# Two-layer hybrid encoder in float32: operand loads moved ahead at the turn to the output projection, one step run ahead of its preparations, and three VectorE and ScalarE jobs spread

## The chip, the cores and the metric

The kernel runs on one core of one Trainium2 chip. A core has TensorE (PE, matmuls; PEld is its weight load), VectorE (DVE), ScalarE (ACT), GpSimd (POOL) and SyncE (SP, which here only issues DMAs). Data lie in SBUF (128 partitions), matmuls accumulate in PSUM banks. The metric is the device time of one execution in microseconds (us); lower is better.

## The reference

One layer is computed on 2048 tokens of width 1024, all in float32: a conditioned RMS norm, one input projection, two kinds of attention with eight heads of 64 each, an output projection with a gated residual, a second norm, and an MLP with a gated residual.

```python
h = rmsnorm(x, g_norm1) * (1 + sc1) + sh1
q_sb, k_sb, v_sb, q_ca, k_ca, v_ca = split(h @ w_in)
o_sb = stick_breaking_attention(q_sb, k_sb, v_sb)             # strictly causal, 8 heads
o_ca = chunked_relpos_attention(rms(q_ca), rms(k_ca), v_ca)   # own chunk + 8 before, 8 heads
x = x + gt1 * (concat(o_sb, o_ca) @ w_o)
h = rmsnorm(x, g_norm2) * (1 + sc2) + sh2
x = x + gt2 * (square(relu(h @ w1)) @ w2)
```

## The kernel before, in words

**Number format.** TensorE multiplies a rounded form of float32. Each operand is therefore split into a rounded high part (a cast, mostly on ACT) and a low part (source minus high, mostly on DVE), and `mm3` (line 211) makes each product from three matmuls: high by high, high by low, low by high. In the MLP the weight is the stationary side, so the third of the three is the first to need the weight's low part.

**Stages.** The tokens stand in four blocks `g` of 512 columns (reversed in time). First come the input projections. Then attention runs unit by unit: SB units (stick breaking; per head and pair of blocks) and CA units (chunked softmax; per head and block), in the order blocks 2 and 3, then 1, then 0. A unit has four steps. In each step DVE scans or reduces one score tile, POOL makes the weights from it, and eight steps later PE transposes the weights, ACT and DVE split them, and PE multiplies them with the values into a bank `acc`. Between these matmuls `fill` (line 1291) puts a share of independent matmuls: projections still to be made, and the output projection `outproj` (line 1155) of blocks 3 to 1. `later.tick()` (line 1401) runs delayed jobs once a step; `soon`, `urgent` and `heavy` are lists of jobs of which each step takes a few.

**Head copies.** When a unit's last value matmul is out, `finish` (line 774) copies one half of `acc` to `otmp` on ACT and puts a second copy, to `o`, on the urgent list; after both POOL adds them. There are two `acc` banks, so the second-next unit's first value matmul needs the two copies. On the last two steps of an SB unit on the diagonal (`short`, line 1391) only jobs beyond the third are taken.

**Norm diagonal.** For blocks 2 and 3 the second norm is made during attention (`finish_row`, line 1186): squares are added up, brought into columns, raised to the power -1/2 on POOL, and then `spread` (line 1215) multiplies the identity with the columns on DVE (`ndgm`), `third` (line 1228) spreads the result over the partitions with matmuls (`prm`) and copies it out.

**The turn.** After attention, four rows of block 1's output projection are left (`row`, line 2097; PE writes `po`). Then eight steps `Mixed` (line 1976; PE writes `pso`) make block 0's output projection. Their moving operands are the eight parts of the attention result, `opm`, loaded from `scr_m[0, k]` by `fetch` (lines 1986 and 2105 to 2112): four ahead of the rows, two after the second row and two after the third, all issued by SP. Parts 4 to 6 are stored by POOL's queue and part 7 by ACT's, shortly before (`keep`, line 798). In the same stretch `right_blocks` (line 1505, called by `some`, line 2091) loads four tiles `ty` (and later `cy`) of the residual stream, multiplies them with the norm on DVE, scales and shifts them on ACT, and forms seven operand tiles `h` of the Strassen-like products of the MLP's first layer. These jobs are written out by hand, block by block (lines 2105 to 2128).

**The MLP.** Its products are lists of steps: `First` (line 1589; seven products, order 1, 5, 6, 3, 7, 2, 4 for each pair of weight tiles), `Second` and `Outer`. The last loop (line 2133) goes through the steps: it first prepares the operands of later steps while there is room for eight tiles, then runs the step's listed jobs (`at`), and then the step's own matmuls. At step 7 it prepares the first two operands of step 8 (`firsts`, shown as `opr`) and makes the four weight sums (`First.fetch`, line 1619; tiles `s`, `ts`, `w`). Step 8 is the first step of `First`; its result is copied by ACT into a second bank (`ps_s<-ps`), on which step 10 goes on. For the second half of the tokens the four weight sums of the first pair are made together six steps before its first step (line 2063).

**Order.** ACT, DVE, POOL and PE instructions, and SP's DMAs from the turn on, keep the order in which the program writes them.

Of the kernel before, what the change touches and what calls it, by code (L numbers as in the profile page):

```python
# [9 lines left out]
F32 = mybir.dt.float32  # L10
# [3 lines left out]
ALU = mybir.AluOpType  # L14
# [4 lines left out]
P = 128  # L19
# [5 lines left out]
KT = D // P  # L25
# [54 lines left out]
def encoder_kernel(ctx, tc, xs, c, g1, g2, w_in, w_first, w_rest, gqk, bias, w_o, w1, w2, w_ada, b_ada, out):  # L80
# [58 lines left out]
    later = Later()  # L139
# [597 lines left out]
    if True:  # L737
# [448 lines left out]
        def finish_row(g, n, ps, xr):  # L1186

            residual(g, n, ps, xr)
            if g < 2 and drain:
                return  # L1190
            stores.pop()()
            if g < 2:
                return

            def square():
                sq = rows[g] if n == 0 else op.tile([P, TB], F32, tag="otmp", name=f"sq{g}_{n}")
                act.activation(sq, xr, AF.Square)
                if n:
                    soon.append(lambda: add(sq))

            def add(sq):
                pool.tensor_tensor(rows[g], rows[g], sq, op=ALU.add)
                if n == KT - 1:
                    later.add(14 if g == 3 else 3, second)

            def second():
                pv = norm_columns(dense, rows[g], f"m{g}")

                def powers():
                    y = norm_powers(op, pv, f"m{g}")  # L1210
                    later.add(2, lambda: spread(y))

                later.add(1, powers)

            def spread(y):
                dg = op.tile([P, TB], F32, tag="otmp", name=f"ndgm{g}").rearrange("p (a b) -> p a b", b=P)

                def part(i):
                    dve.tensor_tensor(
                        dg[:, i : i + 2], ident.unsqueeze(1).to_broadcast([P, 2, P]),  # L1220
                        y[:, i : i + 2].unsqueeze(2).to_broadcast([P, 2, P]), op=ALU.mult,
                    )

                part(0)
                later.add(1, lambda: part(2))
                later.add(3, lambda: third(dg))

            def third(dg):
                pr = dense.tile([P, TB], F32, tag="ps", name=f"prm{g}")
                for i in range(4):  # L1230
                    pe.matmul(pr[:, i * P : (i + 1) * P], ones, dg[:, i, :], start=True, stop=True)
                later.add(1, lambda: dve.tensor_copy(rows[g], pr))

            if n == 0:
                rows[g] = rp.tile([P, TB], F32, tag="r", name=f"r{g}")
            soon.append(lambda: heavy.append(square))
# [123 lines left out]
        for i in range(len(steps) + LAG):  # L1360
            if i % STEPS == 0:
                if i // STEPS + AHEAD < len(units):
                    load(units[i // STEPS + AHEAD])
            vi = i - VST
            if vi >= 0 and vi % STEPS == 0 and vi // STEPS < len(units):
                units[vi // STEPS].load_values()
            front, fs = steps[i] if i < len(steps) else (None, 0)
            back, bs = steps[i - LAG] if i >= LAG else (None, 0)
            done = list(soon)
            soon.clear()  # L1370
            js = []
            if back is not None:
                nb = len(back.blocks)
                js = range(nb * bs // STEPS, nb * (bs + 1) // STEPS)
            for j in js:
                back.transposes(j)
            if front is not None:
                front.soft1(fs)
            while first:
                first.pop(0)()  # L1380
            for j in js:
                back.parts(j)
                late.append((back, j))
            if front is not None:
                front.soft2(fs)
            for job in done:
                if hasattr(job, "bank"):
                    heavy.append(job)
                else:
                    job()  # L1390
            short = front is not None and not front.ca and front.diag and fs > 1
            n = len(urgent) + len(heavy)
            for _ in range(max(0, n - 3) if short else min(n, 1 + (n > 3))):
                (urgent or heavy).pop(0)()
            while len(late) > AVLAG:
                value(*late.pop(0))
            if i + 1 < len(steps):
                u, st = steps[i + 1]
                u.scores(st)
            fill(shares[i], turns.get(i, 0))  # L1400
            later.tick()
# [27 lines left out]
    if True:  # L1429
# [37 lines left out]
        def at(n, job):  # L1467
            jobs.setdefault(n, []).append(job)
# [507 lines left out]
        class Mixed(Step):  # L1976
# [6 lines left out]
                self.tiles = 0 if at else KT  # L1983
                self.frees = KT if at == KT - 1 else 0

            def fetch(self, *ks):
                for k in range(*ks):
                    m = Mixed.parts[k] = opp.tile([P, 2, TB], F32R, tag="op", name=f"opm{self.g}_{k}")
                    sp.dma_start(m.bitcast(F32), scr_m[self.g, k])

            def load(self):
                g, n = self.g, self.n
# [29 lines left out]
        for mb in (1, 0):  # L2022
            begin = len(steps)
            steps += [First(mb, j, i) for j in range(NP) for i in OUTER]
            end = len(steps)
            for j in range(NP):
                f = steps[begin + 7 * j]
                if mb:
                    second_sums(j, begin + 7 * j + 2)
                    if j >= HP:  # L2030
                        narrow_sums(2, j - HP, begin + 71 + 5 * (j - HP))
                else:
                    if j < 12:
                        outer_sums((7, 5, 3)[j // 4], j % 4, begin + 9 * j - 2)
                    if j < HP:
                        for i, n in ((3, 4), (2, 5), (7, 4), (4, 5)):
                            at(begin + 7 * j + n, lambda i=i, f=f: f.other(i))
                    else:
                        narrow_sums(4, j - HP, begin + 65 + 5 * (j - HP))
                if j > mb:  # L2040
                    at(begin + max(7 * j - 13, 2 if mb else -6), f.load)
                if j > mb or mb and j:
                    for m in range(4):
                        at(begin + (m + 1 if mb and j == 1 else 7 * j - 9 + (m if j > 1 else 0)), lambda f=f, m=m: f.fetch(m))
            if mb:
                norm2(1, begin + 18)
                norm2(0, begin + 48)
                for k in range(HK):
                    begins = end + 6 * k
                    pieces = right_blocks(0, k, kept if k % 2 else temp)  # L2050
                    for n, m in ((0, 0), (4, 4), (5, 5), (6, 6), (7, 7), (8, 7), (9, 7), (10, 7), (11, 7), (12, 7)):
                        at(begins + n, pieces[m])
                for i in PLAIN:
                    plain(1, i)
                for n in range(end, len(steps), 2):
                    at(n - 7 - max(0, end + 4 - n) // 2, steps[n].load)
                rest = len(steps)
                lent = lambda nm: rp.tile([P, TB], F32, tag="r", name=nm)
                for n in range(HK):
                    update(1, n, rest + 4 + 12 * n, lent, True)  # L2060
            else:
                at(begin - 8, steps[begin].load)
                at(begin - 6, steps[begin].fetch)

        def plain_loads(f, leads):
            for m in range(0, NP, 2):
# [35 lines left out]
                stores.pop(0)()  # L2102
            return force(left)

        steps[0].fetch(0, KT // 2)
        row()
        row()
        some(0, 0)
        steps[0].fetch(KT // 2, KT - 2)
        row()  # L2110
        some(0, 1)
        steps[0].fetch(KT - 2, KT)
        row()
        some(0, 2)
        some(1, 0)
# [15 lines left out]
        ahead = iter(steps[1:])  # L2131
        nxt = next(ahead)
        for n, s in enumerate(steps):
            while nxt is not None and ready - used + nxt.tiles <= 8 and nxt.ready():
                nxt.prepare()
                ready += nxt.tiles
                nxt = next(ahead, None)
            for m in (0, 1) if n == 0 else (n + 1,):
                if m < KT:
                    steps[m].load_row()  # L2140
            for job in jobs.get(n, ()):
                job()
            if n == KT - 1:
                firsts = spare.tile([P, 2, 2, TB], F32R, tag="r8", name="opr")
                steps[KT].prepare(firsts[:, 0])
                steps[KT].fetch(0)
                steps[KT + 1].prepare(firsts[:, 1])
                for m in range(1, 4):
                    steps[KT].fetch(m)
            s.run()  # L2150
            used += s.frees
            later.tick()
        later.flush()
# [42 lines left out]
```

## Time and profile before

| what | value |
|---|---|
| time, median of 3 runs | 2514.77 us (2513.28 to 2515.25) |
| profiled execution, its own time | 2516.38 us |
| its span in the profile | 2514.6 us |
| busy share of the span: PE, DVE, ACT, POOL | 99%, 81%, 61%, 31% |
| attention ends, PE goes on with `po` alone | 1268.66 us |
| first `Mixed` matmul | 1290.50 us |
| first `First` matmul (step 8) | 1336.53 us |
| first `First` matmul of the second half | 1736.00 us |

The span lacks what lies around the profiled program, here 1.8 us. All times inside the execution are counted from the span's start. In the timeline rows the first number is the start, the second the time until the last of the merged instructions ends, `xN` their count, and a bracket the idle time of the engine before them with what ended it. In the rows of waits stand the total, the number of times and the longest one.

### The profile page before, as it was taken

How to read it: one execution, taken by the hardware profiler on the slowest of the kernel's cores; microseconds unless marked ns; L12 is line 12 of the kernel's file. 1: busy time of each engine (PE TensorE's matmuls, PEld its weight loads, DVE VectorE, ACT ScalarE, POOL GpSimd, SP SyncE). 2: the span in 40 equal slices, each digit the busy share in tenths (PEclk: the TensorE clock that was granted, in tenths of full speed). 3: DMA queues.
4: the chain of work that ended last, by engine and by line, in shares of the span. 5: the costliest groups of instructions: out<-in, count | busy, mean ns of one | idle time of the engine just before them, and what ended most of it. 6: DMA issues, size and time to landing. Idle time of an engine off the chain costs nothing.

```text
span 2514.6 us, 39505 instructions
## 1 busy us (share of the span) xinstructions
PE 2498.9 (99%) x12364; PEld 2094.8 (83%) x12364; DVE 2027.7 (81%) x3567; ACT 1526.4 (61%) x2928; POOL 787.1 (31%) x1174
## 2 busy tenths in 40 slices
PE   9999999999999999999999999999999999999999
PEld 8888888888888888888888888888888888888887
DVE  7656777897799888999858777779877759799998
ACT  6333424778876686666755555567555546577765
POOL 4330154777776677776710000000000000010100
PEclk9999999999999999999999999999999999999999
DMA  9879978789888788866786878996998996888982
GB/s 357 333 297 362 356 269 291 233 262 311 268 262 260 237 259 254 268 195 216 213 323 245 299 285 305 330 351 191 327 323 269 315 363 262 320 249 282 303 280 84
DMA packets 295970, 704.71 MB, mean 280 GB/s; under 512 B 32080, under 2 KB 88400, under 8 KB 284112
## 3 DMA queue, kind: packets, MB, share of 16 engines
q1 hardware_dynamic: 287552, 684.35, 79.3%
q0 software_dynamic: 6768, 13.11, 2.9%
q10 hardware_dynamic: 1440, 4.72, 0.5%
q8 instruction: 98, 1.61, 0.3%
q14 instruction: 112, 0.92, 0.1%
HBM read 473.99 MB, written 228.07 MB: 279 GB/s over the span
## 4 chain that ended last, share of the span: by engine, by line
PE 86%; DVE 5%; DMA 4%; ACT 2%; issue 1%; POOL 0%; SPq 0%; DVEq 0%; ACTq 0%; POOLq 0%
PE ps L42 24%; PE ps_s L42 15%; PE pt L42 11%; PE acc L42 7%; PE wt L42 7%; PE pf L42 6%; PE z L42 5%; PE po L42 4%; PE pq L42 3%; PE cz L42 2%; PE ct L42 1%; DMA scr_t<-twn 1%; DMA hw<-in_w_dram 1%; DVE h L42 1%; DMA opm<-scr_m 1%
## 5 line engine op out<-in xcount | busy, mean ns | idle before, releaser
L42 ACT CAST wth<-wt 128x512 fp32r<-128x512 f32 (+3 forms) x544 | 257.5, 484 | 173.3 <-PE wt L42 160.7
L42 PE MATMUL ps<-h,opw 128*128 128x512 f32 x1512 | 358.6, 389 | 0.0
L42 POOL TENSOR_TENSOR b<-p 128x512 f32<-128x512 f32 (+1 forms) x320 | 291.9, 912 | 155.7 <-DVE p L42 95.6
L42 DVE TENSOR_TENSOR wtl<-wt,wth 128x512 fp32r<-128x512 f32 (+3 forms) x544 | 291.2, 547 | 60.7 <-ACT wth L42 56.2
L42 PEld LDWEIGHTS ps<-h,opw 128*128 128x128 f32 x1512 | 283.6, 188 | 58.9
L42 PE MATMUL pt<-w,ht 128*128 128x512 f32 x1248 | 288.0, 391 | 0.0
L42 PE MATMUL ps_s<-h,opw 128*128 128x512 f32 x1152 | 277.6, 390 | 1.5 <-ACT ps_s L42 1.0
L42 PEld LDWEIGHTS pt<-w,ht 128*128 128x128 f32 x1248 | 232.9, 188 | 47.5
L42 DVE TENSOR_TENSOR_SCAN p<-z,p,zero 128x512 f32<-128x512 f32 x192 | 245.3, 1279 | 20.6 <-ACT z L42 14.9
L42 PEld LDWEIGHTS ps_s<-h,opw 128*128 128x128 f32 x1152 | 215.7, 188 | 47.9 <-ACT ps_s L42 1.4
L42 ACT CAST opr<-r 128x512 fp32r<-128x512 f32 x280 | 174.3, 623 | 118.2 <-PE ps L42 65.6
L42 PE MATMUL acc<-wth,v 128*128 128x512 f32 (+3 forms) x544 | 221.3, 410 | 1.1 <-ACT o L42 1.1
L42 PE MATMUL ps<-opr,ol 128*128 128x512 f32 x960 | 220.3, 389 | 0.0
L42 PEld LDWEIGHTS ps<-opr,ol 128*128 128x128 f32 x960 | 180.1, 188 | 37.8 <-DVE opr L42 0.4
L42 ACT ACTIVATE z<-z 128x512 f32<-128x512 f32 (+1 forms) x320 | 166.6, 521 | 54.3 <-PE z L42 49.9
L42 DVE TENSOR_TENSOR opr<-r,opr 128x512 fp32r<-128x512 f32 x280 | 185.7, 684 | 13.7 <-ACT opr L42 12.5
L42 PE MATMUL acc<-wtl,v 128*128 128x512 f32 (+3 forms) x544 | 185.6, 347 | 0.0
L42 PE MATMUL z<-k,q 128*128 128x512 f32 (+3 forms) x640 | 182.8, 367 | 1.0 <-DVE p L42 0.9
L42 POOL DMA_DIRECT2D scr_x<-txu x12 | 10.4, 866 | 547.7 <-ACT txu L42 545.9
L42 PE MATMUL ps<-oph,opv 128*128 128x512 f32 x768 | 175.7, 390 | 1.2 <-DVE oph L42 0.9
L42 PE MATMUL wt<-ident,b 128*128 128x128 f32 x1088 | 170.7, 272 | 0.4 <-DVE p L42 0.4
L42 PEld LDWEIGHTS ps<-oph,opv 128*128 128x128 f32 x768 | 143.9, 188 | 32.6 <-DVE oph L42 1.4
(238 smaller groups left out, 5062.1 us busy)
## 6 DMA issues: line engine op xcount, KB each, us to landing
r<-scr_hid SPq DMA_DIRECT2D x80, 512.0 KB, 7.4
q<-scr_q SPq DMA_DIRECT2D x128, 256.0 KB, 5.2
w<-in_w_dram SPq DMA_DIRECT2D x64, 512.0 KB, 5.7
k<-scr_k SPq DMA_DIRECT2D x240, 128.0 KB, 4.6
v<-scr_v SPq DMA_DIRECT2D x120, 256.0 KB, 4.6
wa<-in_w_ada_dram SPq DMA_DIRECT2D x48, 512.0 KB, 6.3
ow<-scr_wo SPq DMA_DIRECT2D x24, 1024.0 KB, 6.7
l<-scr_t SPq DMA_DIRECT2D x20, 1024.0 KB, 8.6
```

The lines of the kernel that those rows point to most:

```text
L42: return lambda *x, **y: self.tc.keep_in_program_order(f(*x, **y))
```

## The change

Five edits:

1. **Norm diagonal**: four multiplications of 128x128 in four steps in a row, where there were two of 128x256 in two; `third` comes one step later.
2. **Head copies**: the rule `short` does not hold while the front unit belongs to block 0 and an urgent job waits.
3. **Turn**: parts 0 to 5 of `opm` are fetched by SP ahead of all rows, parts 6 and 7 by ACT's queue directly after that.
4. **First product**: the matmuls of step 8, and the copy behind them, are written ahead of that step's preparations and jobs.
5. **Weight sums**: the second half's first four sums are made one a step, on the steps six to three ahead of its first step.

```diff
@@ finish_row, spread
                 def part(i):
-                    dve.tensor_tensor(
-                        dg[:, i : i + 2], ident.unsqueeze(1).to_broadcast([P, 2, P]),
-                        y[:, i : i + 2].unsqueeze(2).to_broadcast([P, 2, P]), op=ALU.mult,
-                    )
+                    dve.tensor_tensor(dg[:, i], ident, y[:, i : i + 1].to_broadcast([P, P]), op=ALU.mult)
 
                 part(0)
-                later.add(1, lambda: part(2))
-                later.add(3, lambda: third(dg))
+                for i in range(1, 4):
+                    later.add(i, lambda i=i: part(i))
+                later.add(4, lambda: third(dg))
@@ attention loop
-            short = front is not None and not front.ca and front.diag and fs > 1
+            short = front is not None and not front.ca and front.diag and fs > 1 and not (front.g == 0 and urgent)
@@ Mixed
-            def fetch(self, *ks):
+            def fetch(self, *ks, queue=sp):
                 for k in range(*ks):
                     m = Mixed.parts[k] = opp.tile([P, 2, TB], F32R, tag="op", name=f"opm{self.g}_{k}")
-                    sp.dma_start(m.bitcast(F32), scr_m[self.g, k])
+                    queue.dma_start(m.bitcast(F32), scr_m[self.g, k])
@@ steps of the second half
                 at(begin - 8, steps[begin].load)
-                at(begin - 6, steps[begin].fetch)
+                for m in range(4):
+                    at(begin - 6 + m, lambda f=steps[begin], m=m: f.fetch(m))
@@ the turn
-        steps[0].fetch(0, KT // 2)
+        steps[0].fetch(0, KT - 2)
+        steps[0].fetch(KT - 2, KT, queue=act)
         row()
         row()
         some(0, 0)
-        steps[0].fetch(KT // 2, KT - 2)
         row()
         some(0, 1)
-        steps[0].fetch(KT - 2, KT)
         row()
@@ last loop
         for n, s in enumerate(steps):
+            if n == KT:
+                s.run()
             while nxt is not None and ready - used + nxt.tiles <= 8 and nxt.ready():
...
-            s.run()
+            if n != KT:
+                s.run()
             used += s.frees
             later.tick()
```

## Prediction

> **What bounds the kernel now.** I read the page's busy shares first, then PE's waits, then the timelines around the places that the diff touches.
>
> ```profile
> PE 2498.9 (99%) x12364; PEld 2094.8 (83%) x12364; DVE 2027.7 (81%) x3567; ACT 1526.4 (61%) x2928; POOL 787.1 (31%) x1174
> ```
> ```profile
> PE pso L42 <- DMA opm<-scr_m: 1.9, 2, 1.6
> ...
> PE acc L42 <- ACT o L42: 1.1, 1, 1.1
> PE ps_s L42 <- ACT ps_s L42: 1.0, 1, 1.0
> PE ps L42 <- DVE oph L42: 0.9, 1, 0.9
> PE z L42 <- DVE p L42: 0.9, 2, 0.5
> PE cz L42 <- DVE cols L42: 0.7, 1, 0.7
> ```
>
> PE is busy 99% of the span, and the change removes no matmul. Only PE's holes can be won, and these six waits are the ones it aims at. A wait row counts idle time only; a hole is better measured from start to start, with the pace of matmuls that nothing holds up:
>
> ```profile
> 1268.66 22.00 PE L42 MATMUL po<-fx,ow 128*128 128x512 f32 x96
> 1290.50 4.29 PE L42 MATMUL pso<-opm,ow 128*128 128x512 f32 x18
> ...
> 1336.53 5.81 PE L42 MATMUL ps<-h,opr 128*128 128x512 f32 x24
> 1343.30 3.04 PE L42 MATMUL ps_s<-h,opw 128*128 128x512 f32 x12 [0.96 <-ACT ps_s L42]
> ```
>
> From 1268.66 to 1290.50 are 96 matmuls: 0.2275 us each. The eight `Mixed` steps have 192 of them, 43.68 us, so they could end at 1334.18; `First` begins at 1336.53, a hole of 2.35. Its two steps of 12 end at 1341.99, the next begins at 1343.30: 1.31. With 1.1 for the head copies, 0.5 and 0.7 for the two diagonals, and 1.58 for the weight sums (below), 7.5 us stand at the touched places. That is the most that can be won, 0.30%.
>
> **The change part by part.**
>
> **Head copies: -1.1.** One place fits the new condition: block 0's first diagonal unit, with a CA unit's copies still urgent.
>
> ```profile
> 953.28 0.58 ACT L42 COPY otmp<-acc 64x512 f32<-64x512 f32 x1
> ...
> 955.18 0.58 ACT L42 COPY o<-acc 64x512 f32<-64x512 f32 x1
> ```
>
> PE's wait of 1.1 ends with the second copy (955.76). The rule releases both two steps earlier, some 4 us, well ahead of PE's need at about 954.7. The copies stay two of 0.58 us. ACT is 61% busy and hides them; without that cover each could hold up one sigmoid by 0.58, which reaches PE only if DVE's scan behind it has no spare time. Bounds: -1.3 and -0.5.
>
> **Norm diagonal: -0.2.** Here a row speaks against the change.
>
> ```profile
> 1038.35 1.15 DVE L42 TENSOR_TENSOR ndgm<-ident,nym 128x256 f32<-128x256 f32 x1
> ...
> 1208.68 1.24 DVE L42 TENSOR_TENSOR ndgm<-ident,nym 128x256 f32<-128x256 f32 x1
> ```
> ```profile
> 1038.18 1.04 POOL L42 TENSOR_TENSOR b<-p 128x512 f32<-128x512 f32 x1
> ```
> ```profile
> 1208.39 1.25 POOL L42 TENSOR_TENSOR e<-e,cols 128x640 f32<-128x640 f32 x1 [1.68 <-DVE wtl L42]
> ```
>
> The instruction takes 1.15 and 1.24 us. Both times it ends 0.28 us after POOL's instruction does (1039.50 after 1039.22; 1209.92 after 1209.64). So the cost is waiting for POOL, and 0.28 is the work. Half the width saves about 0.14 of each of the first two parts, which fall on the same steps as before; the other 0.8 to 1.1 stays. Two more parts follow, each of which can wait up to 1.25 again. The holes of 0.5 and 0.7 thus shrink by about 0.14 each, of which I leave 0.1 to the extra parts: -0.2. The ends: -1.2 (0.5 + 0.7) if no part waits, and +0.9 if the two extra parts of one diagonal wait some 1.1 each and DVE has only 1.3 to spare before a score bank is late. The matmuls `prm` only move one step.
>
> [...]
>
> **Turn: +0.7.** What SP does there:
>
> ```profile
> 1260.72 1.85 SPq L42 DMA_DIRECT2D opm<-scr_m  x4
> ...
> 1283.85 0.33 SPq L42 DMA_DIRECT2D txr<-in_xs_dram  x1
> 1284.24 1.85 SPq L42 DMA_DIRECT2D ty<-scr_x  x4
> ```
> ```profile
> 1275.90 0.33 ACTq L42 DMA_DIRECT2D scr_m<-os  x1
> ```
> ```profile
> SPq L42 <- DMA scr_m<-os: 9.1, 1, 9.1
> ```
> ```profile
> ow<-scr_wo SPq DMA_DIRECT2D x2, 1024.0 KB, 7.4
> ...
> scr_m<-os ACTq DMA_DIRECT2D x1, 512.0 KB, 7.9
> ```
>
> A `txr` waits 9.1 us for ACT's store of part 7, which it does not read: 1275.90 + 7.9 = 1283.8. In program order it is the eighth DMA of SP and ACT behind that store (four `opm`, `ow`, `txr`, `ow`, `txr`). I read this as a ring of eight completion counters: each DMA waits for the one eight before it. After the change the order is store 7, parts 0 to 5, parts 6 and 7 (ACT), `ow`, `txr`, `ow`, `txr`, then four `ty`. The four `ty` stand eight behind parts 4, 5, 6 and 7. The fourth `ty` now waits for part 7 to land, and part 7 waits for its store at 1283.8.
>
> ```profile
> L42 SPq DMA_DIRECT2D ty<-scr_x x4: 424/430/432, 1284.2 to 1285.7; - x4
> ...
> DMA to landing us min/median/max: 3.5/4.8/5.4
> ```
> ```profile
> opm<-scr_m SPq DMA_DIRECT2D x8, 512.0 KB, 7.4
> ```
> ```profile
> 1290.32 1.44 DVE L42 TENSOR_TENSOR ty<-ty,r 128x512 f32<-128x512 f32 x2 [0.38 <-DMA ty<-scr_x]
> ...
> 1328.19 1.29 DVE L42 TENSOR_TENSOR h<-cy,h 128x512 fp32r<-128x512 f32 x2 [1.05 <-ACT h L42]
> ...
> 1336.32 0.68 DVE L42 TENSOR_TENSOR opr<-w,opr 128x512 fp32r<-128x512 f32 x1
> ```
>
> Part 7, issued near 1283.9, lands after 3.5 us (the fastest `ty`, half its bytes) to 7.4 (the median `opm`, in full traffic); I take 4.4, nearer to the quiet end since the traffic has been moved ahead. 1288.3, then 3.4 for the fourth `ty`: 1291.7. Before, the last two multiplications ended at 1290.32 + 1.44 = 1291.76 and one takes 0.7, so DVE began with the fourth near 1291.0. So the operand chain starts 0.7 later.
>
> Does that count? From 1291 to 1337 DVE and ACT hand each other the 28 tiles `h`; DVE's idle stretches end with ACT (the row at 1328.19 shows the longest, 1.05), ACT's with DVE, none with PE. The chain ends with `opr` at 1336.32 + 0.68 = 1337.00. PE's third matmul of `First`, the first to need it, falls at 1336.53 + 2 x 0.2275 = 1336.99. PE and the chain meet there with nothing to spare. So when the 2.35 of waiting for `opm` go, PE arrives at 1334.2 and waits for `opr` instead, some 3 us. The gain is hidden anyway; the chain's shift is what remains. Also moved: SP now stands still for part 5 until the store of it lands, which POOL issues near 1262 (about 1270 by the 7.9 of a store), with `ow` behind it, issued near 1271 and landed near 1278.5 by its 7.4; PE needs it at 1268.66 + 48 x 0.2275 = 1279.6. If it is late, the 3 us that PE waits later cover it. ACT's queue stands still for part 7 until 1283.8; behind it wait the scalings of `ty`, of which the first comes near then, since `ty` is issued from 1275 on; so this costs nothing. Bounds: -2.35 (the chain keeps up) and +2.5 (part 7 takes 6.2).
>
> **First product: -1.2.**
>
> ```profile
> 1339.66 1.35 ACT L42 CAST opw<-ts 128x512 fp32r<-128x512 f32 x2 [1.41 <-PE ps L42]
> ...
> 1342.67 0.57 ACT L42 COPY ps_s<-ps 128x512 f32<-128x512 f32 x1
> ```
>
> Step 8's product is ready at 1336.53 + 12 x 0.2275 = 1339.26, but its copy stands behind five casts and ends at 1343.24. Written first, it ends near 1339.9, two us before PE needs it, and the hole of 1.31 goes. The price: the casts start 0.3 later. Step 10's weight is due at 1342, with its cast done near 1340.5 and DVE's low part by 1342.2, just ahead of its third matmul at 1342.4; I leave 0.1 for that. Bounds -1.3 and -0.6. It holds whether or not `First` itself begins later.
>
> **Weight sums: -1.5.**
>
> ```profile
> 1726.88 0.68 DVE L42 TENSOR_TENSOR s<-w 128x512 f32<-128x512 f32 x1
> ...
> 1729.53 0.68 DVE L42 TENSOR_TENSOR oph<-hw,oph 128x512 fp32r<-128x512 f32 x1
> ...
> 1736.16 1.28 DVE L42 TENSOR_TENSOR opw<-ts,opw 128x512 fp32r<-128x512 f32 x2
> ```
> ```profile
> 1724.64 4.69 PE L42 MATMUL ps<-oph,opv 128*128 128x512 f32 x20
> 1730.27 5.89 PE L42 MATMUL ps<-oph,opv 128*128 128x512 f32 x23 [0.93 <-DVE oph L42]
> 1736.00 5.60 PE L42 MATMUL ps<-h,opw 128*128 128x512 f32 x24
> ```
>
> Four sums stand in DVE's queue ahead of `oph`. 1724.64 + 20 x 0.2275 = 1729.19, PE goes on at 1730.27 (1.08), and 23 matmuls later another 0.50 is lost. With one sum ahead instead of four, `oph` starts 3 x 0.66 = 2.0 us sooner, at 1727.6. Each later step's low parts then have one sum less of a lead: 1.3 and 0.7 us sooner, and none from the fourth step on, where PE is 1.58 earlier. There the weights of the third and fourth product of `First` are ready at 1737.44, and PE begins the third at 1736.00 + 24 x 0.2275 = 1741.46, so 4.0 us of lead pay for the 1.58. POOL is idle here, so no sum waits. -1.5; bounds -1.6 and -0.8.
>
> **Sum.** -1.1 - 0.2 + 0.7 - 1.2 - 1.5 = -3.3 us. The profiled execution took 2516.38, 1.6 above the median; 2513.1 for it, and 2514.77 - 3.3 = **2511.5** for the median. 0.2% is 5.0 us, about what a measurement of this kernel can tell from no change.
>
> **The rivals.**
>
> *The chain keeps up at the turn* (0.22). If the fourth `ty` comes some 2 us sooner, or the chain has spare time that I don't see, the 2.35 is won: -6.35, 2508.4. For it: the traffic is moved into a stretch where PE and ACT are quiet. Against it: the store of part 7, which nothing moves, still lands ahead of part 7 and `ty`.
>
> *The diagonal's extra parts wait for POOL and PE feels it* (0.15). +0.9 in place of -0.2: 2512.6. For it, all of the long `ndgm` rows; against it, DVE's spare time on later steps.
>
> *The turn makes it slower than before* (0.08). The store of part 7 shares the DMA engines with all that is moved ahead of it.
>
> ```profile
> 1268.00:1274.00 6.00, 6.00 (x30) 4.85 (x29) 1.07 (x3) 2.18 (x5) 4.47 (x4) 1.00 1.02 401
> 1274.00:1280.00 6.00, 6.00 (x28) 4.99 (x27) 0.88 (x2) 0.50 (x1) 1.29 (x1) 1.00 0.92 310
> ```
>
> In these two windows they are 1.02 and 0.92 busy. Two parts, a `txr` and two `ty`, 1.75 MB, go ahead of it; at 401 GB/s that is 4.4 us. If all of it is served before the store, the chain starts 0.7 + 4.4 = 5.1 later: -4.0 + 5.1 = +1.1, 2515.9. It decides from 3.3 us of delay of the store.
>
> *The copies don't come sooner* (0.05), because the urgent list is empty on those steps: 2512.6.
>
> **Chances and range.** The forecast has 0.50, from 2510 to 2513.5. The range takes in the first rival at its lower end and stops short of the third: 2508.3 to 2514.9. Faster by over 0.2% (below 2509.7) is most of the first rival and the forecast's edge: 0.25; slower by over 0.2% needs more than the third rival gives: 0.03; within, 0.72.
>
> **What would show it.** PE's wait for `opm` gone and one of about 3 us for `opr` at `First`'s begin; the fourth `ty` issued when part 7 lands; no wait for `o`, `ps_s` and `oph`; the four narrow `ndgm` ending just after POOL's instructions, with PE's waits for `p` and `cols` nearly as before. I am wrong if `First` begins 2 us earlier in the span, counted from the last attention matmul, or if narrow `ndgm` take 0.2 to 0.3 us.

## The result, and the profile after

| | kernel before | changed kernel |
|---|---|---|
| median (range) of 22 runs each | 2514.5 us (2511.33 to 2516.20) | 2516.92 us (2513.92 to 2520.13) |
| profiled execution, its span | 2516.38, 2514.6 | 2515.57, 2513.9 |

The ratio is 1.0013, 95% interval 1.0007 to 1.0019: the changed kernel is 2.4 us slower. The forecast was 3.3 us faster.

The two profiled executions alone would say 0.7 us faster. Each is one draw from a spread of 5 to 6 us, and the first lies above its median, the second below. So the medians give the total, and the profile gives the places.

PE's waits in the changed kernel (total, times, longest):

```profile
PE po L42 <- DMA ow<-scr_wo: 5.5, 1, 5.5
```

Of the six waits that the change aimed at, four (`opm`, `o`, `ps_s` behind ACT, `oph`) are gone, and those for `p` and `cols` are shorter. At the head of the list stands one that the kernel before did not have: the third of block 1's last four rows, row 6, waits 5.5 us for its weight tile `ow`. PE's timeline at the turn:

```profile
1266.83 11.12 PE L42 MATMUL po<-fx,ow 128*128 128x512 f32 x48
1283.47 12.83 PE L42 MATMUL po<-fx,ow 128*128 128x512 f32 x48 [5.52 <-DMA ow<-scr_wo]
1296.13 16.48 PE L42 MATMUL pso<-opm,ow 128*128 128x512 f32 x72
...
1339.65 5.60 PE L42 MATMUL ps<-h,opr 128*128 128x512 f32 x24
1345.09 2.88 PE L42 MATMUL ps_s<-h,opw 128*128 128x512 f32 x12
```

PE's rows at the begin of the second half:

```profile
1719.75 15.58 PE L42 MATMUL ps<-oph,opv 128*128 128x512 f32 x68
1735.16 5.60 PE L42 MATMUL ps<-h,opw 128*128 128x512 f32 x24
```

Read from stage to stage against the rows of before:

- Attention ends at 1266.83, before at 1268.66: -1.83.
- From there to the begin of `First` 72.82 us, before 67.87: +4.95. The wait is 5.7 from start to start. Behind it 48 matmuls take 12.66 (1283.47 to 1296.13), which at 0.2275 would be 10.92: another 1.74. From this 7.4 the 2.35 for `opm` come off, since `pso` now runs through.
- From there to the second half 395.51, before 399.47: -3.96. No hole is left at step 10 (1345.09 stands 24 x 0.2267 behind 1339.65) and none for `oph`.
- From there to the end 778.74, before 778.6.

Why `ow` came late is read in SP's timeline of the changed kernel:

```profile
1270.05 0.32 SPq L42 DMA_DIRECT2D opm<-scr_m  x1
1276.97 0.32 SPq L42 DMA_DIRECT2D ow<-scr_wo  x1
...
1278.88 4.79 SPq L42 DMA_DIRECT2D ty<-scr_x  x4
```

ACT's timeline beside it:

```profile
1274.08 0.33 ACTq L42 DMA_DIRECT2D scr_m<-os  x1
1274.67 2.60 ACTq L42 DMA_DIRECT2D opm<-scr_m  x2
```

That store among the DMAs from 1255 to 1292 (count, KB each, median us from issue to landing):

```profile
scr_m<-os ACTq DMA_DIRECT2D x1, 512.0 KB, 2.8
```

And SP's waits in the same window:

```profile
SPq L42 <- DMA scr_m<-os: 14.8, 2, 8.3
...
SPq L42 <- DMA ow<-scr_wo: 4.8, 2, 2.9
```

ACT issues the store of part 7 at 1274.08. It lands 2.8 later, at 1276.9, and in that moment SP issues `ow`. SP waits twice for a store of `scr_m`, 14.8 us in all: 8.3 ahead of part 5, which reads what POOL stored, and 6.5 ahead of `ow`, which reads nothing of the kind. So, by the reading that the prediction gave the 9.1 us of `txr` (each DMA waits for the one eight before it), `ow` stands eighth behind the store of part 7. The last row bears it out: the fourth `ty` waits 2.9 us for `ow`, its own place eight before, and is issued at 1283.35 as `ow` lands.

The clock in the same stretch (window, PE busy and count, PEld, DVE, ACT, POOL, then PEclk, DMA share, GB/s):

```profile
1278.00:1283.00 5.00, 0.00 (x0) 0.00 (x0) 0.00 (x0) 0.00 (x0) 0.00 (x0) 0.72 0.97 346
1283.00:1287.00 4.00, 3.53 (x8) 2.81 (x9) 0.75 (x1) 0.00 (x0) 0.00 (x0) 0.50 1.02 409
1287.00:1291.00 4.00, 4.00 (x19) 3.30 (x18) 2.22 (x4) 1.74 (x3) 0.00 (x0) 0.99 0.97 321
```

When `ow` lands, PE goes on at half its clock (0.50) until 1287: 8 matmuls in the 3.5 us in which 15 fit. That is the 1.74.

### The profile page after: what moved, and what is told of

Read it like the earlier page. It is cut to its first block, busy times and chain, and to the rows that moved or that the text cites. A ratio compares the mean times of both kernels' runs of the same rounds, so it can differ in the third digit from the quotient of the medians.

```text
span 2513.9 us, 39512 instructions
## 1 busy us (share of the span) xinstructions
PE 2497.9 (99%) x12364; PEld 2096.0 (83%) x12364; DVE 2028.7 (81%) x3571; ACT 1525.7 (61%) x2928; POOL 787.0 (31%) x1174
## 4 chain that ended last, share of the span: by engine, by line
PE 89%; DVE 4%; DMA 3%; ACT 2%; issue 1%; SPq 0%; POOL 0%; DVEq 0%; ACTq 0%; POOLq 0%
PE ps L42 24%; PE ps_s L42 15%; PE pt L42 11%; PE acc L42 8%; PE wt L42 7%; PE pf L42 6%; PE z L42 5%; PE po L42 5%; PE pq L42 3%; PE cz L42 2%; PE pso L42 2%; PE ct L42 1%; DMA hw<-in_w_dram 1%; PE px L42 1%; DMA scr_t<-twn 0%
## 5 line engine op out<-in xcount | busy, mean ns | idle before, releaser
L42 PE MATMUL po<-fx,ow 128*128 128x512 f32 x576 | 164.2, 397 | 5.5 <-DMA ow<-scr_wo 5.5
```

The lines of the kernel that those rows point to most:

```text
L42: return lambda *x, **y: self.tc.keep_in_program_order(f(*x, **y))
```

## The experiments

**The theories.** *A*: the late `ow` is the loss, through its place in the ring. *B*: another edit lost the time, or something that the profiled execution does not show. Each kernel ran on a chip with runs of the kernel before beside it; "against before" means those. The intervals are some 2.2 us to either side, so differences below that are read from the profiles.

### The changed kernel without the turn's edit, and the turn's edit alone

```diff
-        steps[0].fetch(0, KT - 2)
-        steps[0].fetch(KT - 2, KT, queue=act)
+        steps[0].fetch(0, KT // 2)
         row()
         row()
         some(0, 0)
+        steps[0].fetch(KT // 2, KT - 2)
         row()
         some(0, 1)
+        steps[0].fetch(KT - 2, KT)
```

> The changed kernel with the turn's edit taken back; the other four edits stay. Theory A (the weight tile ow of row 6 stood eight DMAs behind the store of part 7, and its late landing costs all that the other edits gain and more): no wait for ow, 96 matmuls of po again at 0.2275 us, the wait for opm of about 1.6 us is back, attention still ends 1.8 us sooner than in the kernel before; -1.8 - 1.2 - 1.5 = -4.5 against the kernel before, some 2510.0 us; 6 to 7 us below the changed kernel's median of 2516.9 if its stall is usually as long as in its profile. Theory B (the loss comes from one of the four other edits, or from something that the profiled execution does not show): 2514.5 us or more, less than 2 us below the changed kernel.

Measured 2511.15 us, -2.8 against before (2513.91), ratio 0.9991 (0.9982 to 1.0000). That is 5.8 below the changed kernel's median, and 5.2 when each of the two is counted against its own runs of the kernel before.

For the turn's edit alone on the kernel before:

> The kernel before with the turn's edit alone. Theory A: a wait of PE for ow of 4 to 6 us in the third row of po, then some 3.4 us of matmuls at 0.43 us each; no wait for opm; stall 5.7 + slow matmuls 1.7 - opm 2.35 = +5.0, about 2519.5 us. Theory B: within 1.5 us of the kernel before, 2513 to 2516.

Measured 2519.89 us, +6.0, ratio 1.0025 (1.0015 to 1.0034), with the wait for `ow` at the same row:

```profile
1285.70 13.70 PE L42 MATMUL po<-fx,ow 128*128 128x512 f32 x48 [5.55 <-DMA ow<-scr_wo]
```

The turn's edit costs 5 to 6 us with or without the others, so theory B falls. The 48 matmuls behind the wait take 13.70 us here, 12.83 in the changed kernel and 11.12 at full pace, so this second loss varies: 2.6 us here, 1.7 there. The other four together bring 2.8, not the 4.0 of the prediction's terms. Where the rest is, the profile of the kernel without the turn's edit shows. PE:

```profile
1333.95 5.78 PE L42 MATMUL ps<-h,opr 128*128 128x512 f32 x24
1339.57 2.88 PE L42 MATMUL ps_s<-h,opw 128*128 128x512 f32 x12
...
1346.60 3.02 PE L42 MATMUL ps_s<-h,opw 128*128 128x512 f32 x12 [1.43 <-ACT cp L42]
1349.46 2.88 PE L42 MATMUL ps<-h,opw 128*128 128x512 f32 x12
```

ACT in the same kernel:

```profile
1343.13 0.62 ACT L42 CAST opw<-w 128x512 fp32r<-128x512 f32 x1 [2.40 <-DMA w<-in_w_dram]
1345.44 0.62 ACT L42 CAST opw<-ts 128x512 fp32r<-128x512 f32 x1 [1.69 <-DVE ts L42]
1345.97 0.58 ACT L42 COPY cp<-ps_s 128x512 f32<-128x512 f32 x1
```

The hole at step 10 is gone, and two products later PE waits 1.43 us for the copy `cp`, which stands behind two casts, of which the first waits for a load of `w`.

### Without the turn's edit and without that of the first product

The diff is against the kernel without the turn's edit.

```diff
-            if n == KT:
-                s.run()
...
-            if n != KT:
-                s.run()
+            s.run()
```

> Without the turn's edit and without that of the first product (head copies, diagonal and weight sums alone). Theory A (the first product's 1.3 us came back at the fourth product, where PE waits 1.4 us for a copy cp that stands behind casts on ACT): the wait of 1 us for ps_s of step 10 is back at 1340, that of 1.4 us for cp at 1345 is gone; 2511.2 us as without the turn's edit alone, within 0.5. Rival (the edit of the first product is worth its 1.2 us, and the wait for cp has another cause): the wait for cp stays too, 2512.4 us.

Measured 2510.67 us, -3.7 against before (2514.37), ratio 0.9987 (0.9978 to 0.9996). The span is 2509.3, with the edit 2509.2. PE's rows:

```profile
1332.99 6.01 PE L42 MATMUL ps<-h,opr 128*128 128x512 f32 x24
1339.98 3.01 PE L42 MATMUL ps_s<-h,opw 128*128 128x512 f32 x12 [0.99 <-ACT ps_s L42]
...
1345.69 3.02 PE L42 MATMUL ps_s<-h,opw 128*128 128x512 f32 x12
1348.55 2.88 PE L42 MATMUL ps<-h,opw 128*128 128x512 f32 x12
```

The wait at step 10 is back, the one for `cp` is gone, and the span is the same. From `First`'s begin to the product behind the one that needs `cp` PE takes 15.56 us (1332.99 to 1348.55), with the edit 15.51 (1333.95 to 1349.46). Written ahead, the first product brings PE sooner to the next late thing, and no more.

### Parts 4 to 7 on POOL's queue

```diff
-        steps[0].fetch(0, KT - 2)
-        steps[0].fetch(KT - 2, KT, queue=act)
+        steps[0].fetch(0, KT // 2)
+        steps[0].fetch(KT // 2, KT, queue=pool)
```

> The changed kernel, but parts 0 to 3 of opm are fetched by SP as in the kernel before and parts 4 to 7 by POOL's queue, so ow of row 6 stands fifth and ow of row 7 seventh behind the store of part 7. Theory A: neither ow waits, PE waits neither for ow nor for opm. By the second half of the prediction's step (chain of h tiles meets PE with nothing to spare) PE then waits 2 to 4 us for opr at the begin of First, and the time is that of the kernel without the turn's edit, within 1 us: about 2510. By the rival (the chain keeps up) no wait for opr over 0.5 us and 2.3 us less, about 2507.7. If ow still comes late by 5 us, theory A's order of DMAs is wrong: about 2517.

Measured 2514.03 us, ratio 1.0001 (0.9992 to 1.0010). No wait for `ow`, none for `opm`. `First` begins like this:

```profile
1334.96 0.73 PE L42 MATMUL ps<-h,opr 128*128 128x512 f32 x2 [2.45 <-ACT opr L42]
1336.43 6.79 PE L42 MATMUL ps<-h,opr 128*128 128x512 f32 x22 [0.73 <-DVE opr L42]
```

A window of the same kernel:

```profile
1336.00:1340.00 4.00, 3.57 (x9) 2.85 (x10) 3.27 (x6) 0.62 (x1) 0.00 (x0) 0.57 0.17 66
```

The 2.45 and 0.73 us of waiting for `opr` are the "some 3 us" of the prediction. The rival by which the chain keeps up is out. The time is not that of the kernel without the edit, though, but 2.9 us more. The window shows a cost that nobody had counted: PEclk 0.57, with a DMA share of 0.17. Behind this wait, too, matmuls run at half pace, for (1 - 0.57) x 4 / 0.5 = 3.4 us: from 1336.43 to 1343.06 stand 22 matmuls, 6.63 us in place of 5.0, so it costs 1.6. Between the two profiles (2511.5 and 2509.2), counted from start to start at 0.2267 a matmul, that makes 3.6 for `opr` and 1.6 of half pace, less 1.6 for `opm`, 1.7 for `cp` and 0.2 of small holes, which are gone: +1.7 of the 2.3.

### One place in the ring

```diff
-        steps[0].fetch(KT - 2, KT, queue=act)
+        steps[0].fetch(KT - 2, KT, queue=pool)
```

The kernel above changed the place of `ow` and the early traffic at once. This one leaves six parts early.

> The changed kernel with one thing different: parts 6 and 7 are fetched by POOL's queue and not by ACT's. Parts 0 to 5 stay ahead on SP, with all their traffic. That takes one DMA out of the ring between the store of part 7 and ow of row 6, so ow stands seventh behind it and the txr after it eighth. Theory A (the place in the ring alone makes ow late): ow of row 6 is issued between 1266 and 1271 and lands by 1278, no wait for it over 0.5 us; now txr waits for the store, so ow of row 7 is issued right after the store's landing, near 1277.5, lands near 1284 and costs a wait of up to 1.5 us near 1283; then some 3 us for opr. About 2514, like the kernel with parts 4 to 7 on POOL. Rival (the six early parts fill the DMA engines and ow is late for that): a wait of 3 us or more for ow of row 6 stays, 2516 to 2517.

Measured 2514.87 us, ratio 1.0004 (0.9994 to 1.0014). SP in this kernel:

```profile
1269.02 0.38 SPq L42 DMA_DIRECT2D ow<-scr_wo  x1
1278.96 0.33 SPq L42 DMA_DIRECT2D txr<-in_xs_dram  x1
1279.39 0.56 SPq L42 DMA_DIRECT2D ow<-scr_wo  x1
```

PE:

```profile
1277.75 5.72 PE L42 MATMUL po<-fx,ow 128*128 128x512 f32 x24 [0.19 <-DMA ow<-scr_wo]
1287.29 8.58 PE L42 MATMUL po<-fx,ow 128*128 128x512 f32 x24 [3.82 <-DMA ow<-scr_wo]
```

With the same six parts ahead, row 6's `ow` is issued 8 us sooner and PE waits 0.19. `txr`, now the eighth, waits for the store, and row 7's `ow` behind it in SP's queue comes 3.82 us late. The stall moved by one row as the ring moved by one place: the place is the cause, the traffic of the early parts is not. The size was off: the store landed 1.4 us later than assumed and `ow` took 7.8 us to land, not 6.5, so the stall is 3.8, not up to 1.5. Two things went otherwise than expected and nearly cancel. Behind the stall 24 matmuls take 8.58 us, the 24 before them 5.72, so the slower pace costs another 2.9. And PE then waits for no `opr`, where 3 us were expected.

### PE kept busy through the wait

```diff
+                if g == 1 and n == 6:
+                    for _ in range(22):
+                        pe.matmul(ps, mx[0][:, 0, :P], mx[0][:, 0, :], start=True, stop=True)
```

> The changed kernel with 22 extra matmuls (22 x 0.2275 = 5.0 us) on tiles that lie in SBUF already, written ahead of row 6 of block 1's output projection into the bank that the row then begins anew; the outputs are those of the reference. They fill PE's wait for ow. If the half pace behind the wait comes from the idleness: PEclk stays at 1.00 and the matmuls behind ow's landing run at 0.2275 us; First begins 1.4 to 1.8 us sooner against ow's landing; about 1.7 us below the changed kernel, 2515.2. If the half pace comes from the traffic in the same microseconds: 0.43 us again, and the time as the changed kernel, 2516.9. If ow lands earlier than in the profiled execution, the extra matmuls cost up to 5 us themselves.

Measured 2514.77 us, 2.15 below the changed kernel's median (1.6 when each is counted against its own runs of the kernel before); against before 1.0008 (0.9999 to 1.0017). Two windows of this kernel:

```profile
1278.00:1283.00 5.00, 5.00 (x23) 3.81 (x21) 0.00 (x0) 0.00 (x0) 0.00 (x0) 1.00 1.00 391
1283.00:1287.00 4.00, 2.99 (x14) 2.49 (x14) 0.75 (x1) 0.00 (x0) 0.00 (x0) 1.00 1.00 380
```

PE's rows from `ow`'s landing on:

```profile
1284.02 11.18 PE L42 MATMUL po<-fx,ow 128*128 128x512 f32 x48 [1.01 <-DMA ow<-scr_wo]
...
1338.55 5.60 PE L42 MATMUL ps<-h,opr 128*128 128x512 f32 x24
```

`ow` lands within 0.7 us of the changed kernel's. The clock stays at 1.00 in the same DMA traffic (share 1.00), and `First` begins 54.5 us behind the landing, in the changed kernel 56.2 (1283.47 to 1339.65). So in this stretch idleness, not traffic, makes the half pace (0.50 in the changed kernel); it costs 1.7 us here, and 22 useless matmuls buy it back.

### The kernel before once more

> The kernel before, unchanged, run once more with a profile of its own. Its profiled execution took 2516.4 us, 2.4 us over the median of 32 runs (2513.9). If this lies in the execution and not in the profile: the median is again 2513.9 within 0.7 us, and a second profile shows a span of 2511 to 2513 with smaller holes at the places where the first one has 1.1 us and more (the copies at 954, opm at 1294 to 1297, the weight sums at 1729, ps_s at 1962).

Measured 2514.13 us (ratio 0.9998, 0.9990 to 1.0007), span 2511.1, 3.5 below that of the first profile. PE's rows in this second profile:

```profile
1295.17 0.96 PE L42 MATMUL pso<-opm,ow 128*128 128x512 f32 x3 [1.59 <-DMA opm<-scr_m]
1296.42 13.32 PE L42 MATMUL pso<-opm,ow 128*128 128x512 f32 x51 [0.29 <-DMA opm<-scr_m]
...
1336.78 5.60 PE L42 MATMUL ps<-h,opr 128*128 128x512 f32 x24
1342.22 2.88 PE L42 MATMUL ps_s<-h,opw 128*128 128x512 f32 x12
...
1732.72 5.60 PE L42 MATMUL ps<-h,opw 128*128 128x512 f32 x24
```

One window of it:

```profile
1296.00:1300.00 4.00, 3.71 (x10) 2.87 (x10) 3.91 (x8) 1.39 (x3) 0.00 (x0) 0.57 1.06 407
```

The waits for `opm` are those of the first profile, 1.59 and 0.29. Here, but not there, the clock halves behind them (13.32 for 51 matmuls, there 11.86). PE then comes late enough to `First` that step 10 has no hole. From `First` to the second half it takes 395.94, where the first profile has 399.47 and the changed kernel 395.51. So of the 3.96 us that the first product and the weight sums seem to win, 3.5 are not there to win in this execution. Against this profile the changed kernel's +2.8 is: +3.45 at the turn (72.82 - 69.37), -0.43 to the second half, +0.36 behind it, and -0.58 up to attention's end, where 1.7 of gain stand against 1.1 lost ahead of the touched places.

### Two single terms

The kernel before with edit 5 alone:

> The kernel before with the edit of the weight sums alone. The prediction's term was -1.5 us, from holes of 1.09 and 0.38 in the first profile of the kernel before; in its second profile the same place shows 0.29. If the first profile was typical: 2512.7. If the second is: no more than 0.4 us, 2513.9; in both cases no wait for oph at the begin of the second half.

Measured 2512.41 us, -2.0 against before (2514.45), ratio 0.9996 (0.9988 to 1.0005): unclear. No wait for `oph`. The kernel before with edits 1 and 2 alone:

> The kernel before with head copies and norm diagonal alone. Theory A, from the profiles: copies 1.2, diagonals 0.24 + 0.27, so attention ends 1.7 us sooner and nothing behind it takes that back: 2512.5. By the prediction's terms -1.3: 2512.9. If the turn's operands come as late as before in the span and not against attention's end, PE waits 1.7 us longer for opm and the time is that of the kernel before, 2514.2.

Measured 2511.20 us, -3.3, ratio 0.9989 (0.9980 to 0.9998). The 1.7 of its holes lies within the interval. Whether the rest is noise, or fewer executions lose clock at `opm` (PE waits 1.3 us there instead of 1.9), was not settled.

### Better than both

First the turn done differently; the diff is against the kernel with parts 4 to 7 on POOL:

```diff
-        steps[0].fetch(0, KT // 2)
-        steps[0].fetch(KT // 2, KT, queue=pool)
+        some(0, 0)
+        steps[0].fetch(0, KT, queue=pool)
         row()
         row()
-        some(0, 0)
-        row()
         some(0, 1)
         row()
         some(0, 2)
+        row()
         some(1, 0)
```

> All five edits' aims, the turn done in another way: SP loads the four ty ahead of everything else at the turn, all eight opm are fetched by POOL's queue, and the multiplications of ty stand one row sooner. Theory A (what counts at the turn is that ow comes in time and that the chain of some 46 us from the last ty to opr begins sooner): ty lands before 1276, the chain begins near 1278 after the second row's residual, opr is ready some 5 us or more before PE needs it; no wait for ow, opm or opr over 0.3 us; 1.4 us (the wait for opm that is left without the turn's edit) below the 2511.15 us measured without the turn's edit: about 2509.8. If the chain is paced by PE's rows and not by ty, PE waits some 3 us for opr again: about 2513. If eight parts on one queue come late, a wait for opm.

Measured 2510.68 us, ratio 0.9988 (0.9979 to 0.9996). DVE begins with `ty` at 1272.61, 15 us sooner than in the changed kernel, and PE waits for none of `ow`, `opm`, `opr`. DVE:

```profile
1272.61 3.16 DVE L42 TENSOR_TENSOR ty<-ty,r 128x512 f32<-128x512 f32 x4
```

PE:

```profile
1331.61 5.89 PE L42 MATMUL ps<-h,opr 128*128 128x512 f32 x24
...
1344.41 3.02 PE L42 MATMUL ps_s<-h,opw 128*128 128x512 f32 x12 [1.47 <-ACT cp L42]
```

Then steps 8, 9 and 10 ahead of their preparations (`if KT <= n <= KT + 2` in place of `n == KT`):

> As the kernel with ty ahead, and the matmuls and copies of steps 8, 9 and 10 are all written ahead of those steps' preparations (before only of step 8). Theory A (a copy that PE's next product needs stands behind casts on ACT, which wait for a load): the wait for cp of 1.4 us near 1345 is gone too, about 1.5 us below the kernel with ty ahead: 2508.3. If the later operands now come too late in their turn, a new wait of up to 1.5 us for opw near 1348 to 1352 and the same time as with ty ahead.

Measured 2510.14 us, ratio 0.9984 (0.9976 to 0.9993). The wait moved on again, as PE's row shows:

```profile
1351.08 3.02 PE L42 MATMUL ps_s<-h,opw 128*128 128x512 f32 x12 [1.22 <-DVE cp L42]
```

Then the load of `w` sooner, on the kernel with `ty` ahead and on the one with three steps ahead:

```diff
+                if mb and j == 1:
+                    at(begin - 1, f.load)
```

> As the kernel with ty ahead, and the weights w of the second pair of First are loaded two steps sooner, which puts the load ahead of two stores of cxr in SP's queue. Theory A (the wait for cp at the fourth product is the wait for this load, through casts and sums that wait for w and stand ahead of the copy): w lands 3 to 5 us sooner against PE, no wait for cp over 0.3 us between 1340 and 1352; 1.6 us below the kernel with ty ahead (2510.7): 2509.1. If the copy only stands behind casts that are late for another reason, the wait of 1.5 us stays and so does the time.

> Both: three steps ahead of their preparations, and w two steps sooner. Theory A: the wait of 1.2 us for cp near 1351 goes as well; 2508.7, 1.4 us below the kernel with three steps ahead. If gains here are handed on from one wait to the next without end, a wait of about the same size stands within the next 20 us, and the time is 2510 again.

Measured 2508.88 us, ratio 0.9978 (0.9970 to 0.9987), and 2508.49 us, 0.9978 (0.9969 to 0.9988). SP issues `w` 11 us sooner (1328.31, ahead of two stores of `cxr`; without the turn's edit 1339.40). The row is of the first of the two:

```profile
1328.31 1.73 SPq L42 DMA_DIRECT2D w<-in_w_dram  x2
```

The waits for `cp` between 1340 and 1352 are gone in both. In the first of the two PE waits 1.4 us for a later `cp`, at 1954; in the second 0.2. The last kernel is the fastest, 6.0 us below the kernel before and 8.4 below the changed one.

## Why the prediction was wrong, point by point

**Turn (+0.7, measured +4.95 in the profile, 5 to 6 in the medians): this step failed.** The reading was borne out: in three kernels the DMA eighth behind the store of part 7 waits for it, `txr` 9.1 us in the kernel before, `ow` 6.5 in the changed one, `txr` 9.5 with the ring moved by one place. Such waits are all that the profiles show of the ring; what keeps its count was not shown. The count was wrong by one place. The prediction put "store 7, parts 0 to 5, parts 6 and 7 (ACT), `ow`", the order of the source. In the program that ran, part 7 is counted behind `ow`. That makes `ow` the eighth behind the store, and the fourth `ty` the eighth behind `ow`, not behind part 7. This order is read from those two waits and from the run that moved the ring by one place; why it departs from the source's, no run shows. The prediction let `ow` wait only behind part 5 in SP's queue and land 1.1 us before its need. It landed 5.5 after. Even by its own count `ow` was ninth, one place from harm, and that margin was not weighed.

**"If it is late, the 3 us that PE waits later cover it."** The wait that goes covers 2.35 of it, but a stall of 5.7 is larger, and the half pace behind it (1.74 here, 2.6 with the turn's edit alone) was no term at all. The trace of before had shown every matmul of the stretch at 0.2275.

**Turn, second half (the gain is hidden by the chain): right.** With `ow` in time and no wait for `opm`, PE waited 2.45 + 0.73 us for `opr`. With the chain started 15 us sooner that wait is 0.2 or nothing.

**The rival on the other side** had the right sign and the wrong mechanism. It let the store of part 7 come late. The store came early, in 2.8 us where before it took 7.9, and still set the time.

**First product (-1.2, measured -0.05 without the turn's edit): wrong.** The copy does come sooner, but the claim that this "holds whether or not `First` itself begins later" looked one wait ahead. The next, for `cp`, stood 1.4 us behind it. In the changed kernel the hole is gone without a successor because PE comes 3.1 us later to this place.

**Weight sums (-1.5): the mechanism right, the size open.** No wait for `oph` in any kernel with the edit. But the hole is some 1.5 us in one profile of the kernel before and at most 0.5 in the other, which lists no wait for `oph`, and the measurement of the edit alone does not tell -2.0 from nothing.

**Head copies (-1.1): right.** The two copies in the changed kernel:

```profile
949.06 0.58 ACT L42 COPY otmp<-acc 64x512 f32<-64x512 f32 x1
...
951.14 0.58 ACT L42 COPY o<-acc 64x512 f32<-64x512 f32 x1
```

The second is out 4.0 us sooner, as forecast, and PE's wait for `o` is gone.

**Norm diagonal (-0.2, measured -0.5): right in kind.** PE's waits for `p` and `cols` there went from 0.5 and 0.7 us to 0.3 and 0.4. Two of the eight narrow parts on DVE:

```profile
1036.89 1.01 DVE L42 TENSOR_TENSOR ndgm<-ident,nym 128x128 f32<-128x128 f32 x1
...
1206.92 0.98 DVE L42 TENSOR_TENSOR ndgm<-ident,nym 128x128 f32<-128x128 f32 x1
```

POOL's instructions beside them:

```profile
1036.71 1.04 POOL L42 TENSOR_TENSOR b<-p 128x512 f32<-128x512 f32 x1
...
1206.50 1.25 POOL L42 TENSOR_TENSOR e<-e,cols 128x640 f32<-128x640 f32 x1 [1.55 <-DVE wtl L42]
```

Half the width still takes 1.01 and 0.98 where it was 1.15 and 1.24. Both end 0.15 us behind POOL's instruction (1037.90 after 1037.75, 1207.90 after 1207.75), where the full width ended 0.28 behind. Of all eight, seven end 0.15 to 0.16 behind an instruction of POOL that had begun before them; the eighth (1041.55, 0.28 us) begins 0.05 ahead of POOL's next, at 1041.60. That the cost is waiting for POOL is read from these ends. The extra parts cost PE nothing that shows.

**The sum.** Terms as measured, the turn's by its edit alone: -1.2 - 0.5 + 6 + 0 - (0.3 to 1.5) = +2.8 to +4.0. The interval of the measured ratio is +1.8 to +4.8 us, the medians' difference +2.4.

## What to carry to other kernels

In this case a DMA waited for the store eight places before it, whatever it read (9.1 us in the kernel before, 6.5 in the changed one). Before DMAs are moved ahead, find out from the waits in the profile which DMA each one waits for, and count as the built program has them, not as the source reads; a margin of one place was none. A stall of PE had a second price here, 1.5 to 2.9 us of slower matmuls behind it in five of the profiles, so a short wait put in the place of a long one can still cost as much, and a wait removed wins only if the next operand in the chain is ready sooner as well. One profiled execution is enough to name the places, but a hole of 1 us should be seen in a second one before it is booked as a gain.

## What the runs showed of the hardware

The clock was not expected to matter. In the changed kernel it stood at 0.50 from 1280.2 to 1287.1, some 6.8 us, around the end of a wait of 5.5. It halved 2.3 us after PE had run out of work (1277.95, the end of its row of 48), and PE had work again 3.2 us after that, so nearly half of the slow stretch fell into the wait itself; the rest cost 1.7 us.

In two other profiles a window of 4 us shows 0.57 between windows of 1.00, which makes 3.4 us at half: with parts 4 to 7 on POOL's queue, behind a wait of 2.45 with 0.73 after it, at a cost of 1.6 us, and in the second profile of the kernel before, behind 1.59 and 0.29, at a cost of 1.5. In the first profile of the kernel before the same two waits left the clock at 1.00 (windows from 1290 to 1304). So how long a wait has to be, these runs do not tell.

For the turn's edit alone (a wait of 5.55) and with the ring moved by one place (3.82) the cost is read from the matmuls behind the wait, 2.6 and 2.9 us; at half pace that would be 5.2 and 5.8 us of slow matmuls, an estimate. The mean granted clock of these two executions is 0.997, as in the changed kernel, where the first profile of the kernel before has 0.999.

The same store of 512 KB from ACT took 7.9 us to land in the kernel before, 2.8 in the changed one and 5.2 with the ring moved by one place. No run was made to tell what sets this.
